# Four edits in a two-layer hybrid backbone: full-row rotary products, vector-only modulation products, and two changes of order

## The chip, the cores and the metric

The kernel runs on one core of a Trainium2 chip. The metric is device time in microseconds of one execution; three executions are timed and their median counts. One more execution is recorded by the profiler, and all rows below come from it. Engines are called by their names: TensorE (PE, with its weight loads PEld), the vector engine (DVE), the scalar engine (ACT), GpSimd (POOL), and SP, which issues the loads.

## The reference

Two layers work on 512 latent tokens and 256 context tokens of width 1024. Layer 0 is a bidirectional gated linear attention (4 heads, keys of 128, values of 256), layer 1 a latent attention (8 heads; low-rank queries of 384 and low-rank keys and values of 256, a rotary key of 64 that all heads share, normalised queries and keys). Behind each stands a gated FFN with a convolution over three tokens (2816 wide). Ahead of every sub-layer stands an RMS norm with shift and scale, behind it a gate; these six vectors per layer and condition come from `silu(cond) @ w + b`.

```
m = jax.nn.silu(cond) @ w + b                      # six chunks of 1024 per layer and condition
q = concat([q_nope, rope(q_pe)]);  k = concat([k_nope, broadcast(rope(k_pe))])
s = einsum('bqhd,bkhd->bhqk', q, k) * scale        # 128 + 64 wide
x = x + g1 * mixer(h, hc);  x = x + g2 * ffn(modulate(x))
```

The context passes through layer 0 as the latent tokens do, and in layer 1 gives keys and values only. All is float32.

## The kernel before, in words

**Precision.** A float32 operand is split into a high and a low part of a fast format, and a product is three (`mm3`, line 403): high by high, high by low, low by high. Each weight tile of 128 x 1024 is loaded by SP into one of three staging buffers, cast by the scalar engine (high part) and subtracted by the vector engine (low part, `split`, line 365) into one of three weight buffers. `weight_order` (line 295) writes down in which order the weights are wanted; `get` (line 357) takes the next one and keeps two loads ahead.

**Order of the work.** Nothing is issued as it is written. `Later` (line 99) records the operations of a stretch. At the end of each memory pool, `flush` (line 207) plans them: each engine takes, of the operations that are ready by a table of costs, the one that was recorded first. A vector operation with two inputs in memory and a GpSimd operation are planned as excluding each other. The order so planned is the order of each engine's queue; stretches can overlap.

**Stages.** The start loads the tokens, norms them and makes the first head's products (up to 82 us). The linear attention runs to about 346 us: TensorE makes the projections of the next head while the chunk products of this head run (`core`, line 876). Woven into it, `ada_chunk` (line 475) makes four chunks of the modulation, 8 tiles of 128 x 1024 each, for two conditions: `ada_dot` (line 449) multiplies such a tile by the condition and sums its rows. For the first condition this is one vector instruction (`junk<-wa,cb`); for the second it is a product on GpSimd, written over the tile, and a sum on the scalar engine. The tile lies in a staging buffer of the weights. Then come the output product, the norm of the latent and then of the context tokens, and the FFN of layer 0 (about 408 to 960 us), whose first two up tiles are made by `ffn_first` (line 1054), first for the latent, then for the context tokens.

`mla_down` (line 1184) opens layer 1: the context's norm, the compression of the queries (three tiles of 128), the rotary tables (two loads, `tables`, line 1113), the compressed keys of the latent tokens (two tiles), the rotary key of the latent tokens, the first two heads' queries (`mla_uq`, line 1262), the rotary key of the context, the compressed keys of the context. The rotary key then goes through its norm and rotation; `finish` (line 1240) transposes it into `kph`, 128 rows (the 64 values twice), and puts what the fast format leaves of them into `kpl`, 64 rows.

The heads follow (about 1026 to 1250 us). A score tile of 128 queries (`mla_scores`, line 1380) has for each of its two column ranges (512 latent and 256 context keys) five products:

```
self.mm3(o, qh[:, ts], ql[:, ts], kh[:, lo:hi], kl[:, lo:hi], True, False)
mm(o, qe[:, ts], kph[:, lo:hi], start=False, stop=False)
mm(o, qe[:64, ts], kpl[:, lo:hi], start=False, stop=True)
```

`qe` holds the rotary queries' high part in its upper 64 rows and the rest in the lower. There are 8 heads of 4 tiles. Output product and FFN of layer 1 take the rest.

Of the kernel before, what the change touches and what calls it, by code (L numbers as in the profile page):

```python
# [8 lines left out]
F32 = mybir.dt.float32  # L9
F32R = mybir.dt.float32r  # L10
# [3 lines left out]
ALU = mybir.AluOpType  # L14
# [84 lines left out]
class Later:  # L99
# [107 lines left out]
    def flush(self):  # L207
        ops, count = self.ops, len(self.ops)
        deps = [set(o[5]) for o in ops]
        users, ready = {}, [0.0] * count  # L210
        for i, o in enumerate(ops):
            for name in o[6]:
                users.setdefault(name, []).append(i)

        for i, o in enumerate(ops):
            for name in o[6]:
                if users[name][0] == i and name in self.tags and name not in self.old:
                    tag, held = self.tags[name]
                    old = None
                    if len(held) == tag.bufs:  # L220
                        old = next((x for x in held if x not in users or users[x][-1] < i), held[0])
                        held.remove(old)
                    held.append(name)
                    self.old[name] = old
        for name, l in users.items():
            old = self.old.get(name)
            start = max(self.done.get(name, 0.0), self.done.get(old, 0.0))
            for i in l:
                deps[i].update(users.get(old, ()))
                ready[i] = max(ready[i], start)  # L230
        needs = [[] for _ in ops]
        for i, d in enumerate(deps):
            for j in d:
                needs[j].append(i)
        left = [len(d) for d in deps]
        queue = {e: [] for e in self.ENGINES}
        heap = {e: [] for e in self.ENGINES}

        def release(i):
            heapq.heappush(queue[ops[i][0]], (ready[i], i))  # L240

        for i in range(count):
            if not left[i]:
                release(i)
        plan, end, switch = [], [0.0] * count, set()
        while any(queue.values()) or any(heap.values()):
            when = {e: max(self.free[e], 0.0 if heap[e] else queue[e][0][0]) for e in self.ENGINES if heap[e] or queue[e]}
            e = min(when, key=when.get)
            t = when[e]
            while queue[e] and queue[e][0][0] <= t + 1e-9:  # L250
                heapq.heappush(heap[e], heapq.heappop(queue[e])[1])
            i = heapq.heappop(heap[e])
            cost, table, shares = ops[i][7:]
            if shares:

                t = max(t, self.port[e])
            if table and table != self.table:
                t, self.table = t + 1.3, table
                switch.add(i)
            self.free[e] = end[i] = t + cost  # L260
            if shares:
                self.port["gpsimd" if e == "vector" else "vector"] = t + cost
            plan.append((t, len(plan), i))
            for j in needs[i]:
                ready[j] = max(ready[j], end[i] + self.after.get((e, ops[j][0]), 0.0))
                left[j] -= 1
                if not left[j]:
                    release(j)
        if len(plan) != count:
            stuck={i for i in range(count) if left[i]>0}  # L270
            i=min(stuck); path=[]
            while i not in path:
                path.append(i); i=min(j for j in deps[i] if end[j]==0.0)
            raise AssertionError("\n".join(f"{i} {ops[i][0]} {ops[i][1]} {sorted(ops[i][6])}" for i in path[path.index(i):]))
        for name, l in users.items():
            self.done[name] = max(end[i] for i in l)
        with self.tc.manual_schedule():
            for _, _, i in sorted(plan):
                engine, op, args, kw, preload = ops[i][:5]
                if preload and i in switch:  # L280
                    self.real.scalar.preload_act_table_set(*preload)
                getattr(getattr(self.real, engine), op)(*args, **kw)  # L282
        self.ops, self.seen = [], {}


class Net:
# [8 lines left out]
    def weight_order(self):  # L295
# [5 lines left out]
        o += [("wog", n) for n in range(8)]  # L301
        for layer in range(2):
            if layer == 1:
                o += [("wmd", n) for n in (0, 1, 2, 3, 4, 5)]
                o += [("wuq", 0, 0), ("wuq", 0, 1)]
                o += [("wmd", n) for n in (5, 3, 4)]
                o += [("wukv", 0), ("wukv", 1)]
                for h in range(1, 8, 2):
                    if h < 7:
                        o += [("wuq", h // 2 + 1, 0), ("wuq", h // 2 + 1, 1), ("wukv", h + 1), ("wukv", h + 2)]  # L310
                o += [("womh", 0, n) for n in range(4)] + [("womh", 1, n) for n in range(4)]
# [146 lines left out]
            nc.gpsimd.tensor_tensor(prod, wa, self.cb[:, c], op=ALU.mult)  # L458
            nc.scalar.activation(prod, prod, AF.Identity, accum_out=col)

    def ada(self, layer, chunk, nt, conds):

        wa = self.ada_load(layer, chunk, nt)
        self.flip ^= len(conds) == 1
        for c in conds:
            self.ada_dot(wa, layer, chunk, nt, c, None if self.flip or len(conds) == 2 and c == 0 else wa)

    def ada_bias(self, layer, chunk, conds):
        nc = self.nc
# [4 lines left out]

    def ada_chunk(self, layer, ch, conds=(0, 1)):
        for nt in range(8):
            self.ada(layer, ch, nt, conds)
            yield 1.0
        self.ada_bias(layer, ch, conds)

# [504 lines left out]
            yield from self.out_part(w, G, (6, 7))  # L985
            self.residual(self.X0[n], G, 0, 2, n, (LAT, CTX))

    def gla_out(self, og, npool):
        nc, a = self.nc, self.a
        O, X = self.O, self.X0  # L990
        for n in range(2, KT):
# [12 lines left out]
        for n in range(2, KT):  # L1004
            run_all(self.lin(ws[n], O, (CTX,), done(n, CTX)))
            self.ahead(min(n - 1, 3))
        self.norm_seg(npool, X, 0, 1, 1, CTX, g, H)
        return X, H

# [6 lines left out]
            )  # L1016


    def ffn(self, X, H, layer, segs, first, tiles, extra, last):
        tc, nc, a = self.tc, self.nc, self.a  # L1020
        n = segs[-1][1]
        with ExitStack() as ctx:
# [5 lines left out]

                self.hold = {("wup", layer, half * NF + i): f for half, i in tiles[3:]}
            zs = {}  # L1030
            self.ffn_first(f, H, layer, segs, first, tiles, zs)
            for gi in range(len(GROUPS)):
                for kind, *x in self.ffn_order(gi):
                    if kind == "up":
# [16 lines left out]
                self.ffn_down(X, layer, last[1:], f0, gs, c, store, ws[c])  # L1051
                self.ahead(min(i + 1, 3))

    def ffn_first(self, f, H, layer, segs, first, tiles, zs):

        ws = [self.get(("wup", layer, half * NF + i)) for half, i in tiles]
        Gs = [self.G("Gu") for _ in tiles]
        for lo, hi in first:
            for j in range(0, len(tiles), 2):
                for k in range(KT):  # L1060
                    ks = slice(k * P, (k + 1) * P)
                    x, y = H[0][k][:, lo:hi], H[1][k][:, lo:hi]
                    for w, G in zip(ws[j : j + 2], Gs[j : j + 2]):
                        self.mm3(G[:, lo:hi], w[0][:, ks], w[1][:, ks], x, y, k == 0, k == KT - 1)
        for (half, i), G in zip(tiles, Gs):
            z = zs.setdefault(i, {})
            z[half] = self.ztile(f, half, segs)
# [116 lines left out]
    def mla_down(self, X, H, g, p, pq, q, npool):  # L1184
# [5 lines left out]
        self.mq = pq  # L1190
        kp = q.tile([P, T], F32, name="kp")
        kt = q.tile([P, 6, 64], F32, name="kt")
        self.norm_seg(npool, X, 1, 0, 1, CTX, g, H)
        self.compress(pq, q, H, "q", (0, 1, 2), (LAT,), L, first=True)
        self.low_rank_scale(pq, "q", 384, 0, L)
        r["tq"], tk, gpe = self.tables(pq, q)
        self.compress(pq, q, H, "kv", (0, 1), (LAT,), T)

        def rotary_key(lo, hi):
            w = self.get(("wmd", 5))[0]  # L1200
# [11 lines left out]
            nc.scalar.copy(k, ps[:, :, :64])  # L1212
            nc.vector.tensor_tensor(k, k, ps[:, :, 64:], op=ALU.add)

        rotary_key(*LAT)
        r["cq"] = [(self.cst["q"]["h"][i], self.cst["q"]["l"][i]) for i in range(3)]
        self.pre = "m"
        run_all(self.mla_uq(q, 0))
        self.pre = "pre"
        rotary_key(*CTX)  # L1220
        self.compress(pq, q, H, "kv", (0, 1), (CTX,), T)
        self.low_rank_scale(pq, "kv", 256, 0, T)
        r["ckv"] = [(self.cst["kv"]["h"][i], self.cst["kv"]["l"][i]) for i in range(2)]

        sq = q.tile([P, 6, 64], F32, name="ksq")
        nc.scalar.activation(sq, kt, AF.Square)
# [8 lines left out]
            nc.vector.tensor_tensor(kr[:, 4:6, j], kt[:, 4:6], gk.broadcast_to([P, 2, 64]), op=ALU.mult)  # L1235
        self.rotate(q, kr[:, 0:4], kt[:, 0:4], tk, 4, "k", nc.vector)
        kph = r["kph"] = p.tile([P, T], F32R, name="kph")
        kpl = r["kpl"] = p.tile([64, T], F32R, name="kpl")

        def finish():  # L1240
            G = self.G("Gkr")
            for b in range(6):
                nc.tensor.transpose(G[:, b * P : (b + 1) * P], kr[:, b].rearrange("p j f -> p (j f)"), self.ident)
            nc.scalar.copy(kph, G[:, :T])
            nc.vector.tensor_tensor(kpl, G[:64, :T], kph[:64].bitcast(F32), op=ALU.subtract)

        return finish

# [131 lines left out]
    def mla_scores(self, p, t, hd, Ps):  # L1380
# [9 lines left out]
        for lo, hi in (LAT, CTX):  # L1390
            o = G[:, lo:hi]
            self.mm3(o, qh[:, ts], ql[:, ts], kh[:, lo:hi], kl[:, lo:hi], True, False)
            mm(o, qe[:, ts], kph[:, lo:hi], start=False, stop=False)
            mm(o, qe[:64, ts], kpl[:, lo:hi], start=False, stop=True)
        st = p.tile([P, 4], F32, tag="st", name="st", bufs=6)
        nc.vector.tensor_reduce(st[:, 0:1], G[:, :T], axis=AX.X, op=ALU.max, negate=True)
        nc.vector.tensor_scalar(st[:, 1:2], st[:, 0:1], scale, None, op0=ALU.mult)
# [87 lines left out]
    def run(self, out):  # L1485
        tc, nc, a = self.tc, self.nc, self.a
        with ExitStack() as ctx:
# [15 lines left out]
            ps1.enter_context(self.phase("1", G=3, m=2))  # L1503
            with tc.tile_pool(name="wog", bufs=1, reuse_waits="tile") as wp:
                self.hold = {("wog", n): wp for n in range(5, 8)}
                X, H = self.gla_out(og, npool)
            og_stack.close()

            jobs = [(ch, nt) for ch in (1, 0, 2, 4, 3, 5) for nt in range(8)]
# [5 lines left out]
                    for ch in range(6):  # L1515
                        self.ada_bias(1, ch, (0, 1) if ch < 2 else (0,))

            for _ in self.ffn(X, H, 0, (LAT, CTX), (LAT, CTX), [(0, 0), (1, 0)], extra, (LAT, CTX)):
                g = self.gain(1, 0, (0, 1))
                H = self.new_H()  # L1520
                self.norm_seg(npool, X, 1, 0, 0, LAT, g, H)
# [155 lines left out]
```

## Time and profile before

| | us |
|---|---|
| median of three executions | 1649.82 (1647.96 to 1650.46) |
| profiled execution | 1651.06 |
| its span, first to last instruction | 1649.3 |
| TensorE busy | 1606.0 (97%) |
| vector engine busy | 1098.8 (67%) |
| scalar engine busy | 710.7 (43%) |
| GpSimd busy | 273.7 (17%) |

Busy time counts an instruction from its start to its modelled end; TensorE's products overlap, so their durations are longer than the steps from one start to the next. The granted clock is TensorE's, 1.00 being 2.4 GHz; its other level in the records is 1.2 GHz. A wait in square brackets is the time for which the engine stood idle ahead of an instruction, with what ended it. All instructions stand under one line (282), since one helper issues them; they are told apart by the names of their tiles.

### The profile page before, as it was taken

What the parts mean: (1) busy time and instruction counts of PE and PEld (TensorE: products, weight loads), DVE (VectorE), ACT (ScalarE), POOL (GpSimd) and SP (SyncE); (2) the same over time, 40 slices, a digit from 0 to 9 for tenths busy, and PEclk for the clock granted to TensorE, in tenths of its full rate; (3) what the DMA queues carried; (4) which work ended last, traced back from release to release, by engine and by line L of the source; (5) the groups of instructions that cost most, each with busy time, mean ns of one, the idle gap of its engine ahead of it and who ended that gap; (6) DMA issues with size and microseconds to landing.
All of it is one profiled execution on the core that took longest, in us unless ns stands there. A gap on an engine that the chain in (4) does not pass through costs nothing.

```text
span 1649.3 us, 22897 instructions
## 1 busy us (share of the span) xinstructions
PE 1606.0 (97%) x9086; PEld 1382.5 (84%) x9086; DVE 1098.8 (67%) x1791; ACT 710.7 (43%) x1235; POOL 273.7 (17%) x161
## 2 busy tenths in 40 slices
PE   7799999999999999999999999999999999999999
PEld 4699899879888888888888878888879888888887
DVE  6797787975777865556545586766776756555554
ACT  3365565633533433333323256666644533333331
POOL 0023332320223311111100012433300000000000
PEclk9999999999999999999999999999999999999999
DMA  9232422351233543434322222000031233333332
GB/s 325 88 115 87 140 99 98 115 185 39 64 128 103 161 139 122 133 115 137 115 77 77 91 86 65 28 28 26 28 114 52 81 99 93 98 93 99 94 98 77
DMA packets 50078, 165.58 MB, mean 100 GB/s; under 512 B 5554, under 2 KB 7346, under 8 KB 49972
## 3 DMA queue, kind: packets, MB, share of 16 engines
q1 hardware_dynamic: 49332, 162.04, 30.0%
q0 software_dynamic: 640, 2.10, 0.3%
q8 instruction: 71, 1.16, 0.3%
q14 instruction: 35, 0.29, 0.1%
HBM read 159.92 MB, written 4.19 MB: 100 GB/s over the span
## 4 chain that ended last, share of the span: by engine, by line
PE 89%; DVE 5%; ACT 3%; POOL 1%; DMA 1%; issue 1%; SPq 0%; POOLq 0%; DVEq 0%; ACTq 0%
PE G L282 65%; PE Gs L282 5%; PE vps L282 3%; PE av L282 2%; PE Gu L282 2%; PE ukv L282 2%; PE uq L282 2%; PE pt L282 1%; PE ops L282 1%; PE stp L282 1%; DVE junk L282 1%; DVE hl L282 1%; DVE wl L282 1%; PE scp L282 1%; PE adp L282 1%
## 5 line engine op out<-in xcount | busy, mean ns | idle before, releaser
L282 PE MATMUL G<-hh,wh 128*128 128x512 f32 (+1 forms) x1416 | 503.2, 356 | 2.1 <-DVE x L282 1.2
L282 PE MATMUL G<-hl,wh 128*128 128x512 f32 (+2 forms) x1416 | 496.4, 351 | 0.5 <-DVE hl L282 0.5
L282 PE MATMUL G<-hh,wl 128*128 128x512 f32 (+1 forms) x1400 | 490.7, 351 | 0.4 <-DVE wl L282 0.4
L282 DVE TENSOR_TENSOR wl<-ws,wh 128x1024 fp32r<-128x1024 f32 (+3 forms) x178 | 225.5, 1268 | 255.8 <-ACT wh L282 253.9
L282 ACT CAST wh<-ws 128x1024 fp32r<-128x1024 f32 (+3 forms) x186 | 189.3, 1019 | 422.9 <-PE G L282 407.3
L282 PEld LDWEIGHTS G<-hh,wh 128*128 128x128 f32 x1416 | 266.3, 188 | 38.8 <-DVE x L282 1.4
L282 PEld LDWEIGHTS G<-hl,wh 128*128 128x128 f32 (+1 forms) x1416 | 266.2, 188 | 35.9 <-DVE hl L282 1.2
L282 PEld LDWEIGHTS G<-hh,wl 128*128 128x128 f32 x1400 | 263.6, 188 | 34.6 <-DVE wl L282 0.8
L282 POOL TENSOR_TENSOR wa<-wa,cb 128x1024 f32<-128x1024 f32 x64 | 171.6, 2684 | 511.3 <-DVE mod L282 222.5
L282 PE MATMUL G<-ph,wh 128*128 128x512 f32 (+1 forms) x512 | 181.9, 355 | 2.8 <-DVE z L282 2.8
L282 PE MATMUL G<-pl,wh 128*128 128x512 f32 (+1 forms) x512 | 182.7, 357 | 0.0
L282 PE MATMUL G<-ph,wl 128*128 128x512 f32 (+1 forms) x512 | 182.3, 356 | 0.0
L282 DVE SCALAR_TENSOR_TENSOR z<-G,vec,z 128x511 f32<-128x511 f32 x248 | 151.2, 651 | 4.2 <-ACT z L282 3.4
L282 DVE CUSTOM_DVE_ANT_0 junk<-wa,cb 128x1024 bf16<-128x1024 f32 x84 | 111.9, 1332 | 60.7 <-DMA wa<-in_wada 60.5
L282 PEld LDWEIGHTS G<-ph,wh 128*128 128x128 f32 x512 | 96.6, 189 | 18.0 <-issue 3.1
L282 PEld LDWEIGHTS G<-pl,wh 128*128 128x128 f32 x512 | 96.8, 189 | 14.2
L282 PEld LDWEIGHTS G<-ph,wl 128*128 128x128 f32 x512 | 96.6, 189 | 13.7
L282 DVE SCALAR_TENSOR_TENSOR x<-G,mod,x 128x512 f32<-128x512 f32 (+1 forms) x112 | 64.9, 610 | 38.2 <-PE G L282 37.8
L282 ACT ACTIVATE wa<-wa 128x1024 f32<-128x1024 f32 x64 | 67.6, 1056 | 52.4 <-POOL wa L282 52.2
L282 ACT ACTIVATE z<-G,vec 128x768 f32<-128x768 f32 (+1 forms) x82 | 72.6, 885 | 16.7 <-PE G L282 16.7
L282 ACT ACTIVATE z<-z 128x768 f32<-128x768 f32 (+1 forms) x44 | 32.6, 740 | 103.1 <-DVE z L282 103.1
L282 DVE SCALAR_TENSOR_TENSOR y<-G,mod,y 128x512 f32<-128x512 f32 (+1 forms) x72 | 49.3, 688 | 19.0 <-PE G L282 18.5
(340 smaller groups left out, 2608.6 us busy)
## 6 DMA issues: line engine op xcount, KB each, us to landing
wa<-in_wada SPq DMA_DIRECT2D x90, 512.0 KB, 3.7
ws<-in_wup SPq DMA_DIRECT2D x88, 512.0 KB, 3.4
ws<-in_wdn SPq DMA_DIRECT2D x44, 512.0 KB, 3.7
ws<-in_win SPq DMA_DIRECT2D x13, 512.0 KB, 3.6
ws<-in_wmd SPq DMA_DIRECT2D x9, 512.0 KB, 3.5
ws<-in_wv SPq DMA_DIRECT2D x8, 512.0 KB, 4.2
ws<-in_wog SPq DMA_DIRECT2D x8, 512.0 KB, 4.4
ws<-in_womh SPq DMA_DIRECT2D x8, 512.0 KB, 5.3
```

Source lines behind the costliest of these rows:

```text
L282: getattr(getattr(self.real, engine), op)(*args, **kw)
```

## The change

1. **Full-row products.** `kpl` gets 128 rows, the lower 64 filled with zeros (a memset and a copy on the vector engine), and the fifth product of a score range runs on all 128 rows of `qe` and `kpl`.
2. **No GpSimd products in the linear attention.** `ada_chunk` makes both conditions' sums on the vector engine. Layer 1's modulation, made during the FFN of layer 0, keeps its GpSimd products.
3. **First FFN tiles ahead of the context norm.** The latent products of the first two up tiles are recorded, with the loads of their weights, ahead of the context's norm, and so in the same plan; their second load fetches one tile less ahead.
4. **Order in `mla_down`.** The tables come first, then the context's norm, the queries' compression and the first two heads' queries, then the compressed keys of the latent and of the context tokens, and the rotary keys of both last. The order of the weights follows.

```diff
-                o += [("wmd", n) for n in (0, 1, 2, 3, 4, 5)]
-                o += [("wuq", 0, 0), ("wuq", 0, 1)]
-                o += [("wmd", n) for n in (5, 3, 4)]
+                o += [("wmd", n) for n in (0, 1, 2)] + [("wuq", 0, 0), ("wuq", 0, 1)] + [("wmd", n) for n in (3, 4)] + [("wmd", n) for n in (3, 4)] + [("wmd", n) for n in (5,)] + [("wmd", n) for n in (5,)]
...
-    def ada(self, layer, chunk, nt, conds):
+    def ada(self, layer, chunk, nt, conds, alone=False):
...
-            self.ada_dot(wa, layer, chunk, nt, c, None if self.flip or len(conds) == 2 and c == 0 else wa)
+            self.ada_dot(wa, layer, chunk, nt, c, None if alone or self.flip or len(conds) == 2 and c == 0 else wa)
...
-            self.ada(layer, ch, nt, conds)
+            self.ada(layer, ch, nt, conds, True)
...
             self.ahead(min(n - 1, 3))
+        early(H)
         self.norm_seg(npool, X, 0, 1, 1, CTX, g, H)
...
+    def ffn_begin(self, H, layer, seg, tiles, ws=None, Gs=None):
+        ws = ws or [self.get(("wup", layer, half * NF + i), ahead=max(2 - j, 0)) for j, (half, i) in enumerate(tiles)]
+        Gs = Gs or [self.G("Gu") for _ in tiles]
+        lo, hi = seg
+        for j in range(0, len(tiles), 2):
+            for k in range(KT):
+                ks = slice(k * P, (k + 1) * P)
+                x, y = H[0][k][:, lo:hi], H[1][k][:, lo:hi]
+                for w, G in zip(ws[j : j + 2], Gs[j : j + 2]):
+                    self.mm3(G[:, lo:hi], w[0][:, ks], w[1][:, ks], x, y, k == 0, k == KT - 1)
+        return ws, Gs
...
-        self.norm_seg(npool, X, 1, 0, 1, CTX, g, H)
-        self.compress(pq, q, H, "q", (0, 1, 2), (LAT,), L, first=True)
-        self.low_rank_scale(pq, "q", 384, 0, L)
         r["tq"], tk, gpe = self.tables(pq, q)
-        self.compress(pq, q, H, "kv", (0, 1), (LAT,), T)
...
-        rotary_key(*LAT)
+        self.norm_seg(npool, X, 1, 0, 1, CTX, g, H)
+        self.compress(pq, q, H, "q", (0, 1, 2), (LAT,), L, first=True)
+        self.low_rank_scale(pq, "q", 384, 0, L)
...
         run_all(self.mla_uq(q, 0))
         self.pre = "pre"
-        rotary_key(*CTX)
+        self.compress(pq, q, H, "kv", (0, 1), (LAT,), T)
         self.compress(pq, q, H, "kv", (0, 1), (CTX,), T)
         self.low_rank_scale(pq, "kv", 256, 0, T)
...
+        rotary_key(*LAT)
+        rotary_key(*CTX)
...
-        kpl = r["kpl"] = p.tile([64, T], F32R, name="kpl")
+        kpl = r["kpl"] = p.tile([P, T], F32R, name="kpl")
+        zero = q.tile([P, T], F32, name="kzero")
+        nc.vector.memset(zero, 0.0)
+        nc.vector.tensor_copy(kpl[64:], zero[64:])
...
-            mm(o, qe[:64, ts], kpl[:, lo:hi], start=False, stop=True)
+            mm(o, qe[:, ts], kpl[:, lo:hi], start=False, stop=True)
...
-                X, H = self.gla_out(og, npool)
+                begun = []
+                X, H = self.gla_out(og, npool, lambda H: begun.append(self.ffn_begin(H, 0, LAT, [(0, 0), (1, 0)])))
```

## Rows read from the trace of the kernel before

**Rows 1.** Busy time by stage: window, its length, busy (instructions), clock, DMA share, GB/s.
```profile
82.00:346.00 264.00, 259.02 (x1685) 234.75 (x1685) 224.05 (x344) 149.60 (x263) 91.23 (x36) 1.00 0.33 113
346.00:400.00 54.00, 51.71 (x265) 44.10 (x266) 26.44 (x41) 17.35 (x25) 2.06 (x2) 0.94 0.30 100
400.00:420.00 20.00, 19.70 (x122) 17.39 (x121) 15.71 (x27) 9.82 (x19) 4.58 (x3) 1.00 0.16 53
...
955.00:1040.00 85.00, 77.69 (x462) 68.15 (x461) 62.73 (x137) 50.26 (x122) 18.29 (x14) 0.96 0.23 69
1040.00:1250.00 210.00, 208.13 (x1281) 173.41 (x1281) 152.44 (x337) 125.16 (x334) 59.44 (x55) 1.00 0.14 45
```

**Rows 2.** Timeline of TensorE, one score tile: start, duration (us), product.
```profile
1228.89 0.40 PE L282 MATMUL Gs<-kh,qh 128*128 128x512 f32 x1
...
1229.59 0.40 PE L282 MATMUL Gs<-kph,qe 128*128 128x512 f32 x1
1229.92 0.50 PE L282 MATMUL Gs<-kpl,qe 64*128 64x512 f32 x1
1230.35 0.39 PE L282 MATMUL Gs<-kh,qh 128*128 128x256 f32 x1
1230.57 0.28 PE L282 MATMUL Gs<-kl,qh 128*128 128x256 f32 x1
1230.69 0.28 PE L282 MATMUL Gs<-kh,ql 128*128 128x256 f32 x1
...
1231.34 0.39 PE L282 MATMUL av<-pth,vh 128*128 128x256 f32 x1
1231.56 0.28 PE L282 MATMUL av<-ptl,vh 128*128 128x256 f32 x1
```

**Rows 3.** Products by shape, 1036 to 1240: count, busy us, mean ns, idle before.
```profile
L282 PE MATMUL Gs<-kpl,qe 64*128 64x512 f32 x32 | 15.9, 497 | 0.0
...
L282 PE MATMUL Gs<-kph,qe 128*128 128x512 f32 x32 | 13.2, 413 | 0.0
...
L282 PE MATMUL Gs<-kpl,qe 64*128 64x256 f32 x32 | 12.2, 381 | 0.0
```

**Rows 4.** Timeline of the vector engine, the remainder of the rotary key.
```profile
1029.88 0.94 DVE L282 TENSOR_TENSOR kpl<-Gkr,kph 64x768 fp32r<-64x768 f32 x1
```

**Rows 5.** GpSimd by shape, 82 to 346.
```profile
L282 POOL TENSOR_TENSOR wa<-wa,cb 128x1024 f32<-128x1024 f32 x32 | 86.2, 2696 | 189.5 <-DVE mod L282 118.6 <-ACT t L282 32.7 <-DVE cf L282 16.4
```

**Rows 6.** Timeline of the vector engine in the linear attention.
```profile
320.83 2.24 DVE L282 TENSOR_SCALAR R<-R,cf 128x256 f32<-128x256 f32 x1
...
324.30 1.23 DVE L282 CUSTOM_DVE_ANT_0 junk<-wa,cb 128x1024 bf16<-128x1024 f32 x1
...
325.45 0.35 DVE L282 TENSOR_SCALAR R<-R,cf 128x256 f32<-128x256 f32 x1
```

**Rows 7.** Vector engine by shape, 82 to 346.
```profile
L282 DVE CUSTOM_DVE_ANT_0 junk<-wa,cb 128x1024 bf16<-128x1024 f32 x32 | 45.1, 1408 | 13.2 <-DMA wa<-in_wada 13.2
...
L282 DVE TENSOR_SCALAR R<-R,cf 128x256 f32<-128x256 f32 x32 | 31.6, 986 | 0.5
```

**Rows 8.** Timeline of TensorE, first up products and the context's column sums.
```profile
407.66 0.39 PE L282 MATMUL Gu<-hh,wh 128*128 128x512 f32 x1
...
413.39 0.50 PE L282 MATMUL ssq<-ones,nacc 128*128 128x1 f32 x4
```

**Rows 9.** Timeline of GpSimd, powers of the queries and the rotary key.
```profile
1014.09 3.21 POOL L282 TENSOR_TENSOR qss<-qss,mhalf 128x16 f32<-128x16 f32 x1 [21.54 <-DVE qss L282]
1017.27 1.63 POOL L282 TENSOR_TENSOR krs<-krs,mhalf 128x6 f32<-128x6 f32 x1
```

**Rows 10.** Waits of TensorE, 955 to 1040: total us, times, longest.
```profile
PE Gkr L282 <- DVE vl L282: 1.7, 1, 1.7
PE css L282 <- DVE cacc L282: 1.3, 1, 1.3
PE ukv L282 <- DVE kpl L282: 1.1, 1, 1.1
```

More of the change, by code (lines that the diff above doesn't have):

```diff
@@ L268, in flush @@
                     release(j)
[L269 to L274, printed above, removed]
+        assert len(plan) == count, "instructions wait for each other"
         for name, l in users.items():
@@ L986, in out_first_end, with gla_out @@
             self.residual(self.X0[n], G, 0, 2, n, (LAT, CTX))
-    def gla_out(self, og, npool):
+    def gla_out(self, og, npool, early):
         nc, a = self.nc, self.a
@@ L1016, in residual, with ffn @@
             )
-    def ffn(self, X, H, layer, segs, first, tiles, extra, last):
+    def ffn(self, X, H, layer, segs, first, tiles, extra, last, begun=None):
         tc, nc, a = self.tc, self.nc, self.a
@@ L1030, in ffn @@
             zs = {}
-            self.ffn_first(f, H, layer, segs, first, tiles, zs)
+            self.ffn_first(f, H, layer, segs, first, tiles, zs, begun)
             for gi in range(len(GROUPS)):
@@ L1052, in ffn, with ffn_first @@
                 self.ahead(min(i + 1, 3))
[L1054 to L1064, printed above, removed]
+    def ffn_begin(self, H, layer, seg, tiles, ws=None, Gs=None):
[9 more added lines that the diff above has]
+        return ws, Gs
+    def ffn_first(self, f, H, layer, segs, first, tiles, zs, begun):
+        ws, Gs = begun or (None, None)
+        for seg in first[1:] if begun else first:
+            ws, Gs = self.ffn_begin(H, layer, seg, tiles, ws, Gs)
         for (half, i), G in zip(tiles, Gs):
@@ L1244, in finish @@
             nc.scalar.copy(kph, G[:, :T])
-            nc.vector.tensor_tensor(kpl, G[:64, :T], kph[:64].bitcast(F32), op=ALU.subtract)
+            nc.vector.tensor_tensor(kpl[:64], G[:64, :T], kph[:64].bitcast(F32), op=ALU.subtract)
         return finish
@@ L1516, in extra @@
                         self.ada_bias(1, ch, (0, 1) if ch < 2 else (0,))
-            for _ in self.ffn(X, H, 0, (LAT, CTX), (LAT, CTX), [(0, 0), (1, 0)], extra, (LAT, CTX)):
+            for _ in self.ffn(X, H, 0, (LAT, CTX), (LAT, CTX), [(0, 0), (1, 0)], extra, (LAT, CTX), begun[0]):
                 g = self.gain(1, 0, (0, 1))
```

## The prediction

> **What bounds the kernel now.** I read the busy time by stage first, then the TensorE timeline inside the stages that the change touches, and then, for the engines whose work is moved, the groups by shape. The stage table [rows 1] shows TensorE busy nearly all the time: in the linear attention (82 to 346 us) 259.02 of 264 us, in the first up products (400 to 420) 19.70 of 20, in the latent attention (1040 to 1250) 208.13 of 210. Only the stage between, the compressions and the start of the heads (955 to 1040), is looser: 77.69 of 85 us, at a granted clock of 0.96. So nothing is won by easing another engine as such. Time is won where TensorE spends more per product than it must, or where it stands still or at the lower clock level. The vector engine is the next: 224.05 of 264 us in the linear attention, 152.44 of 210 in the latent one.
>
> **Full-row rotary products.** A score tile is ten products: three, then the rotary one on 128 rows, then its remainder on 64 rows, once 512 columns wide and once 256. In the timeline [rows 2] three undisturbed steps of 512 columns take 1229.59 - 1228.89 = 0.70 us, so 0.23 each; an undisturbed step of 256 takes 0.12. But from the rotary product to the 64-row one it is 0.33, from the 64-row one to the next 0.43, and the one behind that starts after 0.22 instead of 0.12. From the tile's first start to the second product after it (1231.56) are 2.67 us; five steps at 0.233 and six at 0.12 would be 1.89. So 0.78 us per tile belongs to the two 64-row products. There are 32 tiles [rows 3], 32 of each width: 25.0 us. The change makes these products 128 rows with zeros below; no column is added, so the undisturbed step is the price.
>
> How much of it comes back? The upper end is 25.0 us, if every other step stays. The lower end goes by the modelled durations alone: (497 - 413) ns x 64 = 5.4 us [rows 3]. TensorE is full in this stretch, so what it saves shortens the stage as long as nobody else is late. The vector engine's 152.44 us of 210 become 152 of 187 if 23 us go, the scalar engine's 125.16 of 210 become 125 of 187: 81% and 67%. Both keep room, though a softmax chain will now and then be late where it was just in time. I take 23 us. The remainder tile costs one memset and one copy more on the vector engine, neither in the trace in that form; the nearest row is the subtraction for the same tile, 0.94 us [rows 4], so between 0 and 1.9 us; the memset waits for nothing, so I take 0.
>
> A rule bears on this from both sides. The Trainium skill, "TensorEngine Tiling (Array Packing)", section Tiling Modes, says that a change of the array's tiling mode drains the engine; the rows agree, with lost time both before and behind each 64-row product, and by it all 25 us would return. The same page, section Overview, gives products with a contraction of 64 or less up to twice the speed; by it there is nothing to win, and that is rival B.
>
> **No GpSimd products in the linear attention.** 32 products leave GpSimd, 2696 ns each, 86.2 us in all [rows 5], and 32 vector products come instead, of the form that the vector engine already runs beside them: 1.23 us undisturbed [rows 6], so 32 x 1.23 = 39.4 us more for an engine with 264 - 224.05 = 40 us of idle time in the stage. Against this stands what the GpSimd product does to its neighbours: the scaling of a state took 2.24 us beside one and 0.35 without [rows 6]. Over the stage that scaling means 986 ns x32 and the vector product itself 1408 ns x32 [rows 7]: 32 x (0.986 - 0.35) + 32 x (1.408 - 1.23) = 20.4 + 5.7 = 26.1 us are given back by these two shapes alone, others not counted. So the vector engine is loaded 13 us more at most, 237 of 264. The scalar engine loses 32 sums. A load's buffer is free after two vector products instead of one, the GpSimd product and the scalar sum: SP's queue, which brings weights through the same buffers, moves up.
>
> What is on the path is only what TensorE waits for: 264 - 259.02 = 5.0 us idle here, 54 - 51.71 = 2.3 us at the stage's end (346 to 400), and there (1 - 0.94) x 54 = 3.2 us lost at the lower clock level [rows 1], which follow a stop. So the best is -10.5 us. The worst, while the vector engine keeps its 27 us of room, is a last normalisation that stands behind six vector products more, 6 x 1.23 = 7.4 us. I take -4, the nearer to the small waits that the contention makes.
>
> **First FFN tiles ahead of the context norm.** Nothing is added; on TensorE's queue the 48 latent products of the first two up tiles now stand ahead of the context's column sums. In the trace they already run there: the first starts at 407.66, the column sums come in between at 413.39 [rows 8]. So at best the 0.3 us of idle time go. At worst the sums stand behind all 48: 407.66 + 48 x 0.23 = 418.7, so 5.3 us later than now, and with them the norm chain (vector, GpSimd, scalar, then eight context tiles) and the context products. What hides this are the 24 latent products of the next up tile, 5.5 us, whose weights are the third load fetched ahead. I take 0, ends -0.3 and +5.3.
>
> **Compressed keys ahead; tables ahead.** No product is added: the loads are the same in number, in another order on SP's queue, whose DMA share is 0.23 here [rows 1]; the two table loads move up, and so do their small vector products, which I take as 0 as they already lie between the norm's. The queries' products come before the keys' compression, so their power on GpSimd (3.21 us, with the key's power of 1.63 us right behind it [rows 9]) is done long before the key needs the engine. The rotary key's products now stand behind the compressed keys and cover the wait of their column sums. What can go is what TensorE waits for: 1.3 us for these sums, 1.7 before the key's transposes, 1.1 for the remainder tile [rows 10], in all 85 - 77.69 = 7.3 us idle, and (1 - 0.96) x 85 = 3.4 us at the lower clock level [rows 1]: at best -10.7. What can come: the key's chain starts later by the 48 compression products of 256 columns, 48 x 0.12 = 5.8 us, and everything behind its transposes with it: at worst +5.8. Between these I take -4: the wait for sums (1.3), half of the other idle time there (about 1.4) and one third of the clock's.
>
> **The sum.** -23 - 4 + 0 - 4 = -31 us. The profiled execution took 1651.06 us (span 1649.3 and 1.76 around it), so 1620.1; it lay 1.24 us above the median of the three runs, 1649.82, so for the median 1618.8: I say **1619 us**.
>
> **The rivals.**
> A. The latent attention is bound by its softmax chains once TensorE is quicker. For it: bursts, as the 81% is a mean. Against it: 35 us of room. Half of the gain, 12.5 us: 1649.8 - 12.5 - 4 - 4 = 1629.
> B. The lost time isn't the 64-row form's; the products keep their steps and the full rows bring nothing. Against it: the time is lost around every 64-row product and nowhere else in the tile. 1649.8 - 8 = 1642. By the second rule of the Trainium skill's page "TensorEngine Tiling (Array Packing)" (section Overview) it would come out so.
> C. The rotary key is late: its transposes wait 5.8 us more instead of the 4 saved: 1619 + 9.8 = 1629. For it: the chain is long (transposes, squares, a power, the rotation). Against it: GpSimd and the vector engine are freer by then, and the first head's key products need no rotary key.
> D. Slower: the vector engine becomes the bound of the linear attention. If it gets nothing back from GpSimd's silence, its 39.4 us use up the 40 idle us, and every chain then runs at its pace; priced with all of it on the path, 1649.8 + 39.4 - 23 - 4 = 1662. It decides once the vector engine is busy for the whole of the stage. Against it stand the 26 us that two shapes alone give back.
> E. All stops go as well: -25 - 10 - 9 = 1606.
>
> **How the numbers follow.** Forecast 57% (its own range 1612 to 1626), A 13%, B 5%, C 12%, D 4%, E 9%. The range of 8 in 10 takes in A and C and the bounds of the unknown terms, and leaves out most of E below and B and D above: **1610 to 1637**. Faster by over 0.2%, about what a measurement can tell here from no change: all but D and mixtures of B, C and part of D, 94%; within it 2%; slower 4%.
>
> **What would show it.** Right: the rotary remainder products at about 413 ns on 128 rows and a step of 0.23 and 0.12 around them; the latent attention shorter by some 23 us with TensorE still full; in the linear attention no GpSimd product of 1024 columns, the state's scaling at 0.35 us on average and the vector engine below 240 us busy; no stop of TensorE before the key's transposes above 1.7 us. Wrong: a latent attention that shortens by less than 15 us with waits of the scores for the vector engine; a vector engine over 95% busy before 346 us; a stop of some 5 us before the context's up products or before the rotary key's transposes.

## The result and the profile after

The changed kernel takes 1623.11 us (median of four runs, 1620.63 to 1624.68) where the kernel before takes 1648.89 (four runs, 1646.85 to 1650.46): ratio 0.9843, 95% interval 0.9826 to 0.9860, which is 25.9 us less (23.1 to 28.7). The forecast was 1619 us. In the profiles the changed kernel's operations stand under line 277 instead of 282.

The busy time by stage comes first, cut where TensorE's first and last products of a stage stand: linear attention, its output product, first FFN, compressions and first head, heads. Both kernels are cut at the same work, but for some 40 products that moved from the first row to the second (1688 became 1649, 330 became 370); these two rows are taken together. Columns: window, length, busy time (instructions) of TensorE, its weight loads, vector engine, scalar engine and GpSimd, granted clock, DMA share, GB/s. Before:

```profile
80.00:345.70 265.70, 260.35 (x1688) 235.26 (x1688) 224.17 (x344) 151.30 (x265) 90.93 (x36) 1.00 0.33 112
345.70:407.70 62.00, 59.44 (x330) 51.80 (x330) 31.29 (x49) 20.18 (x30) 2.47 (x3) 0.94 0.31 106
407.70:964.60 556.90, 553.83 (x3194) 487.56 (x3193) 346.29 (x498) 196.35 (x248) 95.42 (x44) 1.00 0.34 112
964.60:1033.60 69.00, 61.68 (x350) 53.48 (x349) 51.86 (x120) 41.27 (x99) 14.96 (x10) 0.97 0.22 64
1033.60:1253.50 219.90, 218.03 (x1336) 181.70 (x1335) 157.09 (x346) 130.83 (x352) 61.73 (x60) 0.99 0.14 44
```

And after:

```profile
81.30:340.60 259.30, 256.61 (x1649) 232.62 (x1650) 206.23 (x403) 118.08 (x203) 6.73 (x4) 0.99 0.37 119
340.60:403.20 62.60, 61.37 (x370) 54.64 (x369) 33.86 (x53) 18.30 (x27) 1.06 (x2) 1.00 0.26 85
403.20:958.90 555.70, 553.32 (x3195) 486.90 (x3194) 347.46 (x498) 196.28 (x248) 92.83 (x44) 1.00 0.34 111
958.90:1027.10 68.20, 61.16 (x350) 52.77 (x349) 53.34 (x121) 41.36 (x99) 15.21 (x9) 0.97 0.22 71
1027.10:1225.80 198.70, 194.16 (x1337) 178.58 (x1336) 156.84 (x347) 130.08 (x352) 62.38 (x60) 1.00 0.16 49
```

The heads give 21.2 us, the linear attention with its output product 327.7 - 321.9 = 5.8, the compressions 0.8, the first FFN 1.2; the stage before them ends 1.3 us later (81.3 instead of 80.0), and behind the heads 0.2 us are gained. In sum the two profiled executions lie 27.9 us apart. The vector engine's time in the linear attention fell from 224.17 to 206.23 us although 30 of the 32 added products lie in that row (62 instead of 32, below and [rows 7]).

A score tile's timeline on TensorE, after (start, duration in us); it answers to [rows 2]:

```profile
1129.39 0.39 PE L277 MATMUL Gs<-kpl,qe 128*128 128x512 f32 x1
1129.62 0.28 PE L277 MATMUL Gs<-kh,qh 128*128 128x256 f32 x1
...
1129.97 0.28 PE L277 MATMUL Gs<-kph,qe 128*128 128x256 f32 x1
1130.09 0.28 PE L277 MATMUL Gs<-kpl,qe 128*128 128x256 f32 x1
1130.21 0.34 PE L277 MATMUL uq<-wh,cqh 128*128 128x384 f32 x1
```

The remainder products now step like any other: 0.23 us for 512 columns, 0.12 for 256, and the product behind them too. By shape (count, busy us, mean ns) they answer to [rows 3]:

```profile
L277 PE MATMUL Gs<-kpl,qe 128*128 128x512 f32 x32 | 12.7, 396 | 0.0
L277 PE MATMUL Gs<-kpl,qe 128*128 128x256 f32 x32 | 9.0, 282 | 0.0
```

The vector engine's two shapes of the linear attention, after, answer to [rows 7]:

```profile
L277 DVE CUSTOM_DVE_ANT_0 junk<-wa,cb 128x1024 bf16<-128x1024 f32 x62 | 75.6, 1219 | 7.6 <-DMA wa<-in_wada 7.4
...
L277 DVE TENSOR_SCALAR R<-R,cf 128x256 f32<-128x256 f32 x32 | 11.2, 351 | 0.2
```

986 ns became 351 and 1408 became 1219: both stand at their undisturbed length [rows 6].

### The profile page after: what moved, and what is told of

The parts are those of the page before. It is cut to its first block, busy times and chain, and to the rows that moved or that the text cites. A ratio compares the mean times of both kernels' runs of the same rounds, so it can differ in the third digit from the quotient of the medians.

```text
span 1621.4 us, 22848 instructions
## 1 busy us (share of the span) xinstructions
PE 1579.9 (97%) x9086; PEld 1378.6 (85%) x9086; DVE 1086.0 (67%) x1857; ACT 675.0 (42%) x1171; POOL 186.3 (11%) x129
## 5 line engine op out<-in xcount | busy, mean ns | idle before, releaser
L277 DVE TENSOR_TENSOR wl<-ws,wh 128x1024 fp32r<-128x1024 f32 (+3 forms) x178 | 217.0, 1220 | 261.6 <-ACT wh L277 259.9
L277 DVE CUSTOM_DVE_ANT_0 junk<-wa,cb 128x1024 bf16<-128x1024 f32 x116 | 149.5, 1289 | 52.3 <-DMA wa<-in_wada 52.0
L277 POOL TENSOR_TENSOR wa<-wa,cb 128x1024 f32<-128x1024 f32 x32 | 83.1, 2603 | 321.3 <-DMA wa<-in_wada 157.1
L277 PE MATMUL vps<-wh,hh 128*128 128x256 f32 x192 | 55.3, 288 | 1.4 <-ACT v L277 0.9
```

## The experiments

Each was timed in five rounds beside the kernel before. The ratio is that of its time to the kernel before's; "us less" is the ratio's distance from 1 times 1650 us, with its interval.

### Each part alone

Four kernels, each the kernel before with one part of the change. The diffs are those of the change, cut to the part.

**Full rows alone.**

```
-        kpl = r["kpl"] = p.tile([64, T], F32R, name="kpl")
+        kpl = r["kpl"] = p.tile([P, T], F32R, name="kpl")     # and zeros below
...
-            mm(o, qe[:64, ts], kpl[:, lo:hi], start=False, stop=True)
+            mm(o, qe[:, ts], kpl[:, lo:hi], start=False, stop=True)
```

> Full-row rotary products alone. Theory: the time was lost in entering and leaving the 64-row form, 0.78 us per score tile; both remainder products now take an undisturbed step (0.23 and 0.12 us) and the latent attention shortens by 21 us, as in the full change, some 4 us of the 25 being taken by new waits: about 1628 us. Rival: the full change's attention was also helped by the new order ahead of it; then the rows alone give clearly less, 15 us or under: 1634 or more.

1630.93 us, ratio 0.9878 (0.9854 to 0.9902): 20 us less (16 to 24). The heads take 198.7 us, as in the changed kernel: this part makes the whole gain there.

**Vector-only products alone.**

```
-            self.ada(layer, ch, nt, conds)
+            self.ada(layer, ch, nt, conds, True)               # no GpSimd product
```

> Vector-only modulation products in the linear attention alone. Theory: freed of GpSimd's products the vector engine is less busy than before though it makes 32 products more, TensorE's stops near the end of the stage go, and the first up product starts 4 to 8 us earlier: about 1643 us. Rival: the start of the first up products 4.4 us earlier came from the FFN edit, in whose plan that stretch lies; then this one alone gives 0 to 1 us: 1648 to 1649.

1641.99 us, ratio 0.9949 (0.9930 to 0.9967): 8.4 us less (5.4 to 11.5), twice the forecast's term.

**First FFN tiles alone.**

```
+        early(H)                                              # ffn_begin on LAT
         self.norm_seg(npool, X, 0, 1, 1, CTX, g, H)
```

> First FFN tiles ahead of the context's norm, alone. Theory: they ran there anyway, no gain: within 1 us of 1649. Rival: the plan of that stretch is better, 2 to 4 us less: 1645 to 1647.

1648.70 us, ratio 0.9986 (0.9968 to 1.0004): 2.3 us less, with zero inside the interval.

**Order of the compressions alone.**

```
-        rotary_key(*LAT)          # ahead of the queries' products
...
+        rotary_key(*LAT)          # behind all compressed keys
+        rotary_key(*CTX)
```

> Order of the latent attention's opening alone. Theory: the wait for the keys' column sums goes, but TensorE waits longer for the rotary key's transposes, and the early query weights delay the latent norm: 0 to 1.5 us less, 1647.5 to 1649. Rival: the order is worth the 4 us that were forecast and was hidden by the other edits: 1645.

1650.27 us, ratio 0.9995 (0.9980 to 1.0010): nothing. The gain is that of the first two parts.

### What the 64-row products cost

The kernel before, with both 64-row products of a tile at its end.

```
-            mm(o, qe[:64, ts], kpl[:, lo:hi], start=False, stop=True)
+        for lo, hi in (LAT, CTX):
+            mm(G[:, lo:hi], qe[:64, ts], kpl[:, lo:hi], start=False, stop=True)
```

> The kernel before, in which the two 64-row products of a score tile are moved to its end, next to each other; nothing else changes and every product is still of 64 rows. Theory (what costs is going into the 64-row form and out of it): a tile goes in and out once where it did so twice, so between one quarter and one half of the 0.78 us of a tile comes back, over 32 tiles 6 to 12.5 us, about 1640 us, and the attention takes 207 to 214 us where it took 219.8. Rival (a 64-row product is slow by itself, whatever stands beside it): no gain, 1650 us. If the products were slow for the operand they wait for, no gain either.

1641.15 us, ratio 0.9946 (0.9924 to 0.9967): 9 us less (5 to 13), and the heads take 209.7 us; the shapes and counts are those of before. A tile of it on TensorE:

```profile
1156.59 0.28 PE L282 MATMUL Gs<-kph,qe 128*128 128x256 f32 x1
1156.80 0.61 PE L282 MATMUL Gs<-kpl,qe 64*128 64x512 f32 x2
1157.35 0.39 PE L282 MATMUL av<-pth,vh 128*128 128x256 f32 x1
1157.57 0.28 PE L282 MATMUL ukv<-wh,ckvh 128*128 128x256 f32 x1
```

Going in takes 0.21 us instead of 0.12; both products and the way out 0.55 instead of 0.23 + 0.12; the product behind 0.22 instead of 0.12. That is 0.09 + 0.20 + 0.10 = 0.39 us, as for one 64-row product alone in the kernel before (0.78 for two, prediction). Counted over the heads' timeline, a 64-row product follows another directly in 29 of 64 cases (other heads' products come between the rest), so 29 x 0.39 = 11.3 us should come back. The window of the heads shows 10.2 less, with TensorE's idle time up by 1.1 (219.90 - 218.03 before, 209.70 - 206.72 here):

```profile
1031.00:1240.70 209.70, 206.72 (x1337) 179.81 (x1336) 157.46 (x347) 130.51 (x352) 62.38 (x60) 1.00 0.14 47
```

So the price is per change of form, not per product or column, and the rival (slow by itself) is out. What is missing at such a change shows in the weight loads of the kernel before, for the tile of [rows 2]:

```profile
1229.36 0.19 PEld L282 LDWEIGHTS Gs<-kph,qe 128*128 128x128 f32 x1
1229.91 0.18 PEld L282 LDWEIGHTS Gs<-kpl,qe 64*128 64x128 f32 x1 [0.37 <-issue]
1230.35 0.19 PEld L282 LDWEIGHTS Gs<-kh,qh 128*128 128x128 f32 x1 [0.25 <-issue]
```

The load for the rotary product runs ahead of it (1229.36, the product at 1229.59). The load for the 64-row product starts only with its product (both within 0.01 us of 1229.92), and so does the load for the product behind it (1230.35). This agrees with the Trainium skill, "TensorEngine Tiling (Array Packing)", section Tiling Modes (a change of the tiling mode drains the engine); whether it is a drain or only the load held back, these rows do not tell apart. The factor of up to two in the same page of the Trainium skill, section Overview, is for small tiles that work independently beside each other. No run here has such tiles, so it was not tested; a 64-row product that runs by itself, as these do, gained nothing (the pair with its way out took 0.55 us where full rows take 0.35).

### Where the vector-only part gains

First, are the 32 added vector products hidden? The kernel before, with the context's products left out in the linear attention on both engines (so the context's first modulation is not computed).

```
-            self.ada(layer, ch, nt, conds)
+            wa = self.ada_load(layer, ch, nt)
+            self.ada_dot(wa, layer, ch, nt, 0)                # condition 0 alone
```

> The kernel before, in which the 32 products of the context's condition in the linear attention are left out altogether, on GpSimd and on VectorE (a zero stands in their place, so the context's first modulation is not computed). Theory (the 8 us of the vector-only part come from VectorE's instructions no longer standing behind GpSimd's, and the 32 products that VectorE took over, some 39 us, lie in its idle time): the same as the vector-only part alone, 1642 us, within 2. Rival (the gain is larger and the added products eat part of it): 1636 us or less, and the stretch from the first to the last product of the linear attention below 255 us.

1640.90 us, ratio 0.9950 (0.9930 to 0.9969), as with the 32 products on the vector engine (0.9949), and the linear attention takes 258.6 us beside 258.1, with its output product 320.7 beside 320.7. The added products cost nothing that shows here; the intervals leave room for some 3 us.

Then, where does the relief pay? TensorE's waits of the kernel before around the end of the linear attention, 310 to 400 us (total, times, longest):

```profile
PE Got L282 <- DVE og L282: 1.5, 1, 1.5
PE stp L282 <- DVE R L282: 1.4, 1, 1.4
PE G L282 <- DVE x L282: 1.2, 1, 1.2
PE G L282 <- ACT hh L282: 0.8, 1, 0.8
PE G L282 <- DVE hl L282: 0.5, 1, 0.5
```

and the stretches ahead of and behind the stops:

```profile
340.00:346.60 6.60, 4.31 (x32) 3.42 (x31) 6.60 (x12) 1.98 (x3) 4.13 (x2) 1.00 0.98 362
346.60:353.40 6.80, 6.29 (x18) 4.77 (x19) 3.43 (x7) 3.25 (x5) 0.46 (x1) 0.52 0.77 289
```

TensorE was busy 4.31 of 6.60 us, and then the granted clock was 0.52 of 2.4 GHz, near its lower level, for 6.8 us: (1 - 0.52) x 6.8 = 3.3 us lost besides the stops. Of the stops, those for `og`, `hh` and `hl` (2.8 us) are for the last heads' normalisation (`orr`, `o`, `og`) and the splits of what it makes; the one for `R` (1.4 us) lies 25 us earlier, at the running state of the linear attention. On the vector engine of the kernel before:

```profile
325.72 3.15 DVE L282 TENSOR_TENSOR hl<-og,hh 128x768 fp32r<-128x768 f32 x1
...
335.66 1.60 DVE L282 TENSOR_SCALAR orr<-ss 128x6 f32<-128x6 f32 x1 [0.93 <-ACT o L282]
...
339.60 3.82 DVE L282 TENSOR_SCALAR o<-o,orr 128x256 f32<-128x256 f32 x6
```

beside these on GpSimd:

```profile
325.67 2.39 POOL L282 TENSOR_TENSOR wa<-wa,cb 128x1024 f32<-128x1024 f32 x1 [2.75 <-DVE mod L282]
334.81 2.42 POOL L282 TENSOR_TENSOR wa<-wa,cb 128x1024 f32<-128x1024 f32 x1 [6.75 <-DVE mod L282]
...
339.66 2.56 POOL L282 TENSOR_TENSOR wa<-wa,cb 128x1024 f32<-128x1024 f32 x1
```

The six-element scaling ends when the GpSimd product does (335.66 + 1.60 = 337.26; 334.81 + 2.42 = 337.23). The split at 325.72, 0.95 us without a neighbour, ends 0.81 us behind its GpSimd product: it looks as if such an instruction does its work only once the product is over. The Trainium skill, "SBUF — State Buffer", section Who interferes with whom, has it so for instructions that need the ports which the two engines share: the one that issues first holds them for its whole instruction, and the other blocks. The power of the same normalisation runs on GpSimd itself and stands behind that product there too (it starts at 337.40), so the two kinds of delay are not told apart at this step.

Two counterparts test whether the end of the stage is what counts: no GpSimd products in the last of the four groups of eight tiles, or none in the first three.

```
-            self.ada(layer, ch, nt, conds)
+            self.ada(layer, ch, nt, conds, ch == 5)           # the counterpart: ch != 5
```

**The last group alone.**

> The kernel before, with the vector engine doing both products alone in the last of the four groups of eight modulation tiles only (the eight GpSimd products from 299 to 345 us in the trace of the kernel before go, the other 24 stay). Theory (the gain of the vector-only part is made at the end of the linear attention, where the last heads' normalisation stands beside GpSimd products, TensorE runs out of other products and its clock falls behind the stop): 6 to 8 us of the 8, 1643 us, no stop above 0.6 us from 310 to 348 us and a granted clock of 0.95 or more there. Rival (the relief is spread over the stage): 8 of 32 products, 2 us, 1648 us, and the stops at the end stay.

1641.18 us, ratio 0.9946 (0.9925 to 0.9967): 9 us less (5 to 12), the whole of the part with 8 of its 32 products. The same normalisation on the vector engine, which starts 4.7 us earlier:

```profile
330.93 0.17 DVE L282 TENSOR_SCALAR orr<-ss 128x6 f32<-128x6 f32 x1
...
334.31 1.67 DVE L282 TENSOR_SCALAR o<-o,orr 128x256 f32<-128x256 f32 x6 [1.21 <-POOL orr L282]
```

Of TensorE's waits from 300 to 400 us only 1.2 and 0.2 are left, and the clock holds behind them:

```profile
346.60:353.40 6.80, 5.57 (x30) 4.65 (x29) 5.86 (x10) 4.10 (x5) 0.00 (x0) 1.00 0.35 127
```

**The first three groups alone.**

> The counterpart: the kernel before, with the vector engine doing both products alone in the first three groups of eight modulation tiles; the eight GpSimd products of the last group stay. Theory (the gain is made at the end of the stage): 0 to 2 us, 1648.5 us, and the stops for the last heads' normalisation and the lower clock behind them stay. Rival (spread): 24 of 32, 6 us, 1643.5 us. A third way: without contention before, the last heads come early enough in spite of it, and the stops go as well: 1643 us with the last normalisation several us earlier.

1649.49 us, ratio 0.9993 (0.9977 to 1.0009): nothing, with 24 of 32 products gone. The normalisation was earlier here (`orr` at 333.62, 0.16 us), as the third way had it, but the remaining GpSimd products, the last of them now at 347.15 and 352.22 us, then stood beside the splits behind it. TensorE's waits, 300 to 400 us:

```profile
PE G L282 <- DVE hl L282: 2.9, 2, 1.5
PE G L282 <- DVE wl L282: 1.5, 1, 1.5
PE G L282 <- DVE x L282: 1.2, 1, 1.2
```

The vector engine and GpSimd of that kernel there:

```profile
343.55 3.46 DVE L282 CUSTOM_DVE_ANT_0 junk<-wa,cb 128x1024 bf16<-128x1024 f32 x1
...
346.94 4.00 DVE L282 TENSOR_TENSOR hl<-og,hh 128x768 fp32r<-128x768 f32 x2
```

```profile
342.57 3.36 POOL L282 TENSOR_TENSOR wa<-wa,cb 128x1024 f32<-128x1024 f32 x1 [6.76 <-DVE mod L282]
347.15 2.98 POOL L282 TENSOR_TENSOR wa<-wa,cb 128x1024 f32<-128x1024 f32 x1 [1.22 <-ACT wa L282]
```

So the stops change their name and stay. What pays is the silence of GpSimd over the last 47 us of the stage (its products of the last group stand from 299 to 347 us in the kernel before); which of the eight matter was not tried. The expectation that the old stops would be seen again was wrong in the place, not in the sum. The clock stayed at 1.00 from 340 to 400 us this time; it stood at 0.66 from 80 to 90 us instead, where the kernel before has 1.00, so one trace does not tell what the clock's share is. And each of these edits also changes the order that is planned for every engine; no run holds that order fixed, so that the held instructions make the loss, and not the order, is read from their rows and not tested.

**The same in the second layer's products.** The changed kernel, without GpSimd products beside the first FFN either.

```
-                    self.ada(1, ch, nt, (0, 1) if ch < 2 else (0,))
+                    self.ada(1, ch, nt, (0, 1) if ch < 2 else (0,), True)
```

> The changed kernel, with the vector engine alone doing the second layer's modulation products too, which lie beside the first FFN: 32 GpSimd products fewer there, and 32 vector products more. Theory (contention costs time only where the vector engine's work is late for TensorE; here TensorE is busy 553.32 of 555.7 us, and full from 500 us on): within 1.5 us of the changed kernel, 1623 us; at best the 2.4 us of idle time before 500 us go. Rival (the removed products pay wherever they stand): 3 us or more, 1620 us or less. Against both: the vector engine's 32 products more make it late, 1626 us.

1626.56 us, ratio 0.9857 (0.9836 to 0.9877) against the changed kernel's 0.9843 (0.9826 to 0.9860): no gain of 3 us. The figure is nearest to the third case, the small loss, but the intervals do not tell it from nothing.

### Why the new order does not bring its 4 us

TensorE's waits from the compressed queries to the first scores, after; they answer to [rows 10]:

```profile
PE Gc L277 <- DVE hl L277: 3.3, 3, 1.9
PE Gkr L277 <- DVE vl L277: 2.9, 1, 2.9
PE kpt L277 <- ACT kp L277: 0.5, 1, 0.5
```

The stop for the column sums (1.3) and that for the remainder tile (1.1) are gone, as forecast; the one ahead of the key's transposes grew from 1.7 to 2.9, the normed context comes later (3.3 where the same list of before has 2.7), and a stop of 0.5 ahead of the first transposes of the rotary key's products (`kpt`) is new: 2.4 us went and 2.3 came. The list names `vl` for the 2.9 us, but the vector engine had ended the key's last instruction (`krr`) just ahead of it, at 1019.80 us, and the transposes start at 1020.12. To see whether the key's late start is the cause, both rotary key parts go ahead of the context's compressed keys (the order of the weight loads follows, not shown):

```
         self.compress(pq, q, H, "kv", (0, 1), (LAT,), T)
+        rotary_key(*LAT)
+        rotary_key(*CTX)
         self.compress(pq, q, H, "kv", (0, 1), (CTX,), T)
```

> The changed kernel, in which both rotary key parts are recorded between the latent and the context's compressed keys, where they were recorded last. Theory (the new 2.9 us stop ahead of the key transposes is the rotary key's vector chain, which starts only with the last products of the stage): the stop goes below 0.6 us, the stretch from the compressed queries to the first scores shortens by 2 to 3 us, 1620.5 us. Rival (TensorE then stops for the context's column sums and their split instead, 1.1 to 1.3 us each in the kernel before): it gains under 1 us, 1622.5 us, with the idle time ahead of the keys' up products above 1.5 us.

1621.90 us, ratio 0.9836 (0.9815 to 0.9857), not to be told from the changed kernel. Its waits in the same stage:

```profile
PE Gc L277 <- DVE hl L277: 3.3, 3, 2.0
PE ukv L277 <- DVE kpl L277: 1.7, 1, 1.7
PE css L277 <- DVE cacc L277: 1.4, 1, 1.4
```

The stop ahead of the transposes is gone, so the late start was its cause; 1.7 + 1.4 us came in its place, where the rival had them. The stage was not shortened: 70.1 us beside 68.2 in the changed kernel, at a granted clock of 0.95 beside 0.97, where 2 to 3 us less were expected. The last run of this question: the changed kernel with the old order.

```
-                o += [("wmd", n) for n in (0, 1, 2)] + [("wuq", 0, 0), ("wuq", 0, 1)] ...
+                o += [("wmd", n) for n in (0, 1, 2, 3, 4, 5)]    # and mla_down as before
```

> The changed kernel with the compression of the second layer and its weight loads in the order of the kernel before; the other three parts stay. Theory (the new order only trades one wait for another): the same as the changed kernel, 1623 us, within 1.5. Rival (the order gains only beside the other parts, as its own run could not show): slower than the changed kernel by 2 us or more, 1625.5 us. A second rival (the order costs): 1621 us.

1625.10 us, ratio 0.9855 (0.9834 to 0.9877); the stage takes 68.5 us beside 68.2. The intervals overlap: whether the order is worth 2 us beside the other parts stays open; the traces show no such difference in the stage.

### Two edits alone

The kernel before with the full rows and without GpSimd products in the last group of eight (both diffs above).

> The kernel before with two edits alone: full-row rotary products, and no GpSimd products in the last of the four groups of modulation tiles. Theory (these two carry the whole gain; the other 24 vector-only products, the FFN's beginning and the order of the compressed keys bring nothing that can be measured): the same as the changed kernel, ratio to the kernel before 0.984, 1623 us, within 2. Rival (the parts that showed nothing alone gain beside the others): 1626 us or more. If the order and the FFN's beginning cost something: 1620 us.

1623.63 us, ratio 0.9834 (0.9813 to 0.9856): 27 us less (24 to 31). Its stages have both gains: 199.2 us for the heads, 320.9 for the linear attention with its output product. Two edits carry the whole gain, as far as the intervals tell; no version here is measurably faster than the changed kernel.

## Why the prediction was right, and where it was off

**Full rows (-23): right, in mechanism and size.** The heads took 21.2 us less, alone and with the rest; the prediction's mechanism, loss at every change of row form, is what the adjacent products show. TensorE's busy time fell by 218.03 - 194.16 = 23.9 us, but its idle time rose from 1.87 to 4.54. The new waits of the heads, after, name the softmax and the next head's keys:

```profile
PE ukv L277 <- DVE kl L277: 1.2, 2, 0.9
PE ukv L277 <- DVE st L277: 1.1, 2, 0.6
PE Gs L277 <- ACT pr L277: 0.9, 2, 0.6
PE pt L277 <- DVE ptl L277: 0.7, 2, 0.3
```

The list of before has `st` at 1.1 and `pr` at 0.3. So rival A exists, at a price of 4.54 - 1.87 = 2.7 us instead of 12.5; rival B fell with the full rows' own run. The factor in the Trainium skill's page, on which B leaned, is not one for a lone product, as said above.

**Vector-only products (-4): the term was mis-sized.** It measured -8.4 (5.4 to 11.5). The step that failed is "I take -4, the nearer to the small waits that the contention makes": the waits that count are not small ones spread over the stage but lie at its end, where, by their rows, instructions held by the last eight GpSimd products delay the last heads, and the lower clock (3.3 us) stood right behind these stops. The bound of -10.5 held for the middle of the measured interval, not for its end. The vector engine's load was mis-sized as well: 237 of 264 us forecast, 206.23 of 259.3 seen. With 30 products of 1.22 us more, some 54 us came back where 26.1 were counted: other shapes were relieved as well (the weights' splits went from 1430 to 1222 ns on average, the sums of keys from 1500 to 952). Rival D lost its condition by that.

**First FFN tiles (0): right.** -2.3 (-5.3 to +0.7), with zero inside. After, the context's column sums start 410.53 - 403.21 = 7.3 us behind the first up product where it was 5.7 [rows 8], and TensorE stops 0.6 us for the normed context.

**Order of the compressions (-4): wrong, it measured -0.8 (-3.3 to +1.7).** The waits for the sums and for the remainder tile did go. The step that failed is to count "half of the other idle time" and a third of the clock's loss as gained too, and the later start of the key's chain at nothing: the chain starts behind the last product of the stage, so its stop grew to 2.9 us, over the 1.7 that the prediction set as its own mark, and the stage's clock is 0.97 before and after. That is rival C, at a price of 1.2 us for that stop and not 5.8. The later context fits what the vector engine shows at 967 us in the changed kernel (the queries' weights, loaded earlier, are split there ahead of the norm's last tiles; in the kernel before at 985), but this was not tried.

**The sum.** -31 forecast, -25.9 (23.1 to 28.7) measured. That it lands so near is in part luck: the vector term was some 4 us too small by its own run and the order term some 3 to 4 us too large, and the two errors nearly cancel. The heads' new waits take about 2 us more. What is left is no larger than what the four parts' intervals leave open.

## What to carry to other kernels

Count how often a stream of products changes its row form; each excursion cost 0.39 us here at 512 and at 256 columns, and zero rows that kept the form took no step more on TensorE. Of an engine's contention ask only what stands beside the last chain of a stage, where TensorE has nothing else to do: here eight of 32 products made all of the gain. In a stage that is a chain of short dependent steps, a moved product takes the wait with it; forecast nothing there until the list of waits after the move is written down.

## What the runs showed of the hardware

An excursion into 64-row products is paid before (0.09 us), at (0.20) and behind (0.10), and two neighbours share it; the weight load at a change of form starts with its product and not ahead of it. A vector instruction held by a GpSimd product did its work only when that product was over, and ended behind it by roughly its own undisturbed length at most: six elements 0.03 us behind (0.17 us became 1.60), 1024 columns 1.08 us behind (347.01 beside 345.93; 1.22 us became 3.46). Not every neighbour was held: the four `og` instructions of the kernel before, which read `Got` as TensorE leaves it, took 2.18 us from 344.49 on beside a GpSimd product from 344.70 on, no more than undisturbed (1.80 + 0.48 where the last group has none). One kernel's runs mostly go with their mean granted clock: the adjacent products took 1632.35 us at 0.994 and 1643.78 at 0.989, a spread wider than three of the four parts' effects. And stops did not always lower the clock: with the first three groups changed TensorE was busy 4.06 of 6.8 us from 346.6 us on, at a clock of 1.00, where the kernel before fell to 0.52 behind 4.31 of 6.6.
